# Large expert places in 32-slot products, another order of places, and an fp32 token gather

## The chip, the cores and the metric

The kernel runs on one core of one Trainium2 chip, in one launch. The metric is the time of an execution in device microseconds. Before the change it is 1484.67 us, the median of three runs (1484.15 to 1487.27).

## The reference

A trunk of two layers works on 256 tokens of 1024 features, all in fp32. Layer 0 has attention and a dense SwiGLU. Layer 1 has dilated attention and then the part that matters here, routed experts: each token goes to 2 of 8 experts, and an expert is a SwiGLU with 3584 hidden features. Cut to that part:

```python
logits = jnp.einsum('td,de->te', xt, router)
top_val, top_idx = lax.top_k(logits, TOP_K)          # TOP_K = 2 of 8 experts
gates = jax.nn.softmax(top_val, axis=-1)
...
def one_block(args):
    tok, g, e = args
    xb = xt[tok]
    yb = (jax.nn.silu(xb @ wg[e]) * (xb @ wu[e])) @ wd[e]
    return (yb.astype(jnp.float32) * g[:, None]).astype(h.dtype)
...
y = jnp.zeros_like(xt).at[tok_pad].add(yb.reshape(P, D))
```

An expert has three weight matrices, together 42 MiB in fp32; all eight are read once in each execution, which is 336 loads of 1 MiB.

## The kernel before

**Places.** The experts are worked on one after the other in eight *places*. Place 0 always takes expert 7 (`FIRST`), so that its loads need no routing result; which expert the other places take is decided on the chip by the number of tokens that each expert has. `TWO` lists the small places, which have room for 64 tokens (slots); the other, large ones have 96. `RANK` says which place the expert of each rank gets, so that the three experts with the fewest tokens go to small places. Tokens beyond the room go through `overflow`, which is skipped when there are none.

**A place.** `expert` first makes the hidden features in seven groups of 512: in each, eight steps of 128 input features (`KD`) for gate and up. Then come 28 steps for the output. Each step uses one *granule*, half of a 1 MiB load `w` (128 partitions x 1024 columns); a place has 84 of them, 42 loads. In `products` (L1283 is its matmul) the gathered tokens `xg` are the stationary operand and the weights stream. The slots of a place stand in `parts`: 64 slots as two products side by side in the array, each 64 columns wide, with half of the weight columns (512) each; and in a large place 32 more slots as four products, each 32 wide, with 256 columns each. The 64-slot products write to `psA` (for the output `psD`), the 32-slot ones to `psB`. TensorE executes one fp32 product as two instructions, each with its weight load.

**Around the products.** After a group ScalarE (silu) and VectorE (the product with up) make `hh`, which `turn` transposes on TensorE into `psC` (L1292) and copies to `ht` for the output steps. The call of `turn` in the code stands behind the fourth step of the next group; the order in which instructions stand on an engine is made by a scheduler when the kernel is built. `scatter` scales the result and adds it to the output in DRAM by an indirect DMA on POOL's queue (L1328), one for the 64 slots and in a large place a second one.

**Routing.** Places are gathered in pairs. `route` makes one-hot tiles `oh` (L1242, VectorE) and multiplies the tokens by them (L1251), which puts the tokens of two places into `xg`; smaller products (L1265) give each slot its gate and row. The tokens stand in `htok` twice: rounded to fp32r (L1101), and what the rounding left, also in fp32r (L1152, `htok_lo`); the gather sums the products of both. Route 0 runs ahead of place 0, and the others within the output steps of places 1, 3 and 5.

**Weights.** Loads are issued by SP in the order of use into 16 slots of 1 MiB; a load waits until its slot's last product is done.

Of the kernel before, what the change touches and what calls it, by code (L numbers as in the profile page):

```python
# [10 lines left out]
F32 = mybir.dt.float32  # L11
F32R = mybir.dt.float32r
BF16 = mybir.dt.bfloat16
I32 = mybir.dt.int32
AF = mybir.ActivationFunctionType
ALU = mybir.AluOpType
AX = mybir.AxisListType

P = 128
D = 1024  # L20
# [2 lines left out]
NE = 8  # L23
EPS = 1e-6
BIG = 4096.0
TWO = (1, 3, 5)
FIRST = NE - 1
RANK = (-1, 0, 3, 1, 4, 2, 5, 6)
ROOM = tuple(64 if j in TWO else 96 for j in range(NE))
RING = 8  # L30
NCONV = 3
# [148 lines left out]
def tile_trunk(ctx, tc, xT_d, fm_d, rw_d, ct_d, ada_et, ada_e, win_ab, win_c, uq_d, ukv_d, wout_e,  # L180
# [910 lines left out]
    cms.close()  # L1091
    ring4 = ctx.enter_context(tc.tile_pool(name="ring4", bufs=RING4, side="right"))
    more.append((slot(ring4), RING4))
    htok = keep.tile([P, 2, 2, D], F32R, tag="h", name="htok")
    yt = token_rstd(st, mb)
    lg = mb.tile([P, 2, NE], F32, name="lg")
    for tt in range(2):
        V.scalar_tensor_tensor(lg[:, tt], pl[tt][:, :NE], yt[:, tt:tt + 1], rb, op0=ALU.mult, op1=ALU.add)
    dump("lg", lg)
    for tt in range(2):  # L1100
        S.activation(htok[:, 0, tt], acc[:, tt], AF.Copy, scale=yt[:, tt:tt + 1])  # L1101
    rank = mb.tile([P, 2, NE], F32, name="rank")
    sel = mb.tile([P, 2, NE], F32, name="sel")
    bsh = [P, 2, NE, NE]
# [43 lines left out]
            for j in range(n):  # L1148
                S.copy(t[j * p:(j + 1) * p], g5[j * p:(j + 1) * p, j * w:(j + 1) * w])

    def htok_lo(tt):
        V.scalar_tensor_tensor(htok[:, 1, tt], acc[:, tt], yt[:, tt:tt + 1], htok[:, 0, tt].bitcast(F32),  # L1152
                               op0=ALU.mult, op1=ALU.subtract)

    def tmp3(name):
        return mt.tile([P, 512], F32, tag="xv", name=name, bufs=2)

    iota = C("iota")
    htok_lo(0)
    pos = mb.tile([P, 2, NE], F32, name="pos")  # L1160
    tot = mb.tile([P, 2, NE], F32, name="tot")
    V.tensor_scalar(pos, sel, -4096.0, 4096.0, op0=ALU.mult, op1=ALU.add)
# [34 lines left out]

    def gates():

        htok_lo(1)  # L1200
        V.tensor_reduce(lm, lg, axis=AX.X, op=ALU.max)
        V.tensor_tensor(gate, lg, lm[:, :, None].to_broadcast([P, 2, NE]), op=ALU.subtract)
        S.activation(gate, gate, AF.Exp)
        V.tensor_tensor(gate, gate, sel, op=ALU.mult)
        V.tensor_reduce(gsum, gate, axis=AX.X, op=ALU.add)
        V.reciprocal(gsum, gsum)
        V.tensor_tensor(gate, gate, gsum[:, :, None].to_broadcast([P, 2, NE]), op=ALU.mult)
        placed(gtok[:, :, :, 0], gate, "pg")
        V.tensor_copy(gtok[:, :, :, 1], C("tok")[:, :, None].to_broadcast([P, 2, NE]))
        t = tmp3("pe")[:, :NE * NE].rearrange("p (a b) -> p a b", a=NE)  # L1210
        V.tensor_tensor(t, perm, iota[:, None, :NE].to_broadcast([P, NE, NE]), op=ALU.mult)
        V.tensor_reduce(key, t, axis=AX.X, op=ALU.add)
        V.tensor_copy(eid, key)
        V.tensor_scalar(cap, rk8, float(len(TWO)) - 0.5, -32.0, op0=ALU.is_lt, op1=ALU.mult)
        V.tensor_scalar(cap[:, :NR], cap[:, :NR], 96.0, None, op0=ALU.add)
        V.memset(cap[:, FIRST:FIRST + 1], float(ROOM[0]))
        V.tensor_tensor(ct8, ct8, cap, op=ALU.subtract)
        V.tensor_scalar(ct8, ct8, 0.0, None, op0=ALU.max)
        V.tensor_reduce(cmax, ct8, axis=AX.X, op=ALU.max)
        V.tensor_copy(cnt[:, 0:8], ct8)  # L1220
        V.tensor_copy(cnt[:, 8:9], cmax)

        st_ = C("stri")
        V.tensor_scalar(side[:, 0:1], st_[:, 64:65], -1.0, 2.0 * BIG + 1.0, op0=ALU.mult, op1=ALU.add)
        V.tensor_tensor(side[:, 1:2], st_[:, 32:33], st_[:, 64:65], op=ALU.add)
        V.tensor_tensor(side[:, 1:2], side[:, 1:2], st_[:, 96:97], op=ALU.add)
        V.tensor_scalar(side[:, 1:2], side[:, 1:2], -1.0, 4.0 * BIG + 3.0, op0=ALU.mult, op1=ALU.add)
# [6 lines left out]
    def route(e, hook=lambda: None):  # L1234

        at = (0, ROOM[e])
        n = ROOM[e] + ROOM[e + 1]
        oh = mt.tile([P, 2, 2 * 96], F32R, tag="oh", name="oh")
        xg = xgp.tile([P, KD, 2 * 96], F32, tag="xg", name="xg")
        for tt in range(2):  # L1240
            for i in range(2):
                V.tensor_scalar(oh[:, tt, at[i]:at[i] + ROOM[e + i]], iota[:, :ROOM[e + i]],  # L1242
                                spos[:, tt, e + i:e + i + 1], None, op0=ALU.is_equal)
        hook()
        for a in range(4):
            ps = bank("C").rearrange("p (a b) -> p a b", a=2)
            for b in range(2):
                d = 2 * a + b
                for i in range(2):
                    for tt in range(2):  # L1250
                        TE.matmul(ps[:, b, :n], htok[:, i, tt, d * P:(d + 1) * P], oh[:, tt, :n],  # L1251
                                  start=tt == 0 and i == 0, stop=tt == 1 and i == 1)
            for b in range(2):
                d = 2 * a + b
                S.activation(xg[:, d, :n], ps[:, b, :n], AF.Identity, bias=sh3[:, d:d + 1], scale=gs3[:, d:d + 1])
        back = []
        for i in range(2):
            back.append([])
            for p, (lo, m, q) in enumerate(parts(e + i)):
                gsl = mt.tile([P, 1], F32, tag="gsl", name="gsl", bufs=8)  # L1260
                row = mt.tile([P, 1], I32, tag="row", name="row", bufs=8)
                ps = bank("C")
                for j in range(q):
                    for tt in range(2):
                        TE.matmul(ps[m * j:m * j + m, 0:2], oh[:, tt, at[i] + lo:at[i] + lo + m].bitcast(F32),  # L1265
                                  gtok[:, tt, e + i], start=tt == 0, stop=tt == 1, tile_position=(0, m * j))
                S.copy(gsl, ps[:, 0:1])
                V.scalar_tensor_tensor(row, ps[:, 1:2], float(q), side[:, p:p + 1], op0=ALU.mult, op1=ALU.add)
                back[i].append((gsl, row))
        return xg, at, back  # L1270

    def expert(e, xg, lo, mid, ahead):
# [5 lines left out]
        def products(outs, x, w, m, start, stop):  # L1278
            for ps, (at, n, q) in zip(outs, parts(e)):
                c = 1024 // m // q  # L1280
                wv = w.rearrange("p (m c) -> p m c", m=m)
                for j in range(q):
                    TE.matmul(ps[n * j:n * j + n, :m * c].rearrange("p (m c) -> p m c", m=m), x(at, n),  # L1283
                              wv[:, :, j * c:(j + 1) * c], start=start, stop=stop, tile_position=(0, n * j))

        def turn(g):

# [12 lines left out]
        for g in range(7):  # L1300
            ps = [bank("A"), bank("B")][:len(parts(e))]
            for k in range(KD):
                products(ps, lambda at, n: xg[:, k, lo + at:lo + at + n], next(wg), 2, k == 0, k == KD - 1)
                if g and k == 3:
                    turn(g - 1)
                if g == 0 and k == 3 and mid:
                    mid()
# [51 lines left out]
def overflow(tc, nc, op, e, cap, off, bank, load, ident, htok, gs3, sh3, pos, gate, iota, g5, acc, gu_d, wd_d):  # L1359
# [13 lines left out]
    for a in range(2):  # L1373
        ps = bank("C").rearrange("p (a b) -> p a b", a=4)
        for b in range(4):
            d = 4 * a + b
            for tt in range(2):
                for i in range(2):
                    TE.matmul(ps[:, b], htok[:, i, tt, d * P:(d + 1) * P].bitcast(F32), oh[:, tt],
                              start=tt == 0 and i == 0, stop=tt == 1 and i == 1)  # L1380
        for b in range(4):
            d = 4 * a + b
            V.tensor_scalar(xg[:, d], ps[:, b], gs3[:, d:d + 1], sh3[:, d:d + 1], op0=ALU.mult, op1=ALU.add)
# [59 lines left out]
```

## Time and profile before

| what | value |
|---|---|
| median of three runs | 1484.67 us (1484.15 to 1487.27) |
| profiled execution | 1487.64 us |
| its span (first to last instruction) | 1485.8 us |
| mean granted TensorE clock in it | 0.984 of 2.4 GHz |
| TensorE busy, products | 1418.4 us (95%) |
| VectorE busy | 433.6 us (29%) |
| ScalarE busy | 354.2 us (24%) |
| POOL busy | 51.1 us (3%) |
| read from HBM | 467.34 MB, 317 GB/s over the span |
| first routed products start | 518.3 us into the span |

The profile is of one execution, which took 1.84 us more than its span. Busy time is the sum of instructions, and products overlap, so that 95% does not say that the array is at its peak; which engine holds up the others has to be read stage by stage.

### The profile page before, as it was taken

To read this page: it belongs to the slowest core of one execution; us is meant where nothing else is said; L and a number is where in the kernel's file an instruction comes from. 1 tells how busy PE (TensorE), PEld (TensorE's weight loads), DVE (VectorE), ACT (ScalarE), POOL (GpSimd) and SP (SyncE) were. 2 spreads that over 40 slices of the span, in tenths; PEclk is the share of its full clock that TensorE was granted. 3 is DMA by queue.
4 is the path that set the end of the run, shared out by engine and by line. 5 is a ranking of instruction groups with operands and counts; after the bars stand their busy time and mean duration, and the time that the engine had idled before them with its cause. 6 is when DMAs were issued, how large, how long until landed. Compare 5 with 4: busy or idle time off the path is not lost.

```text
span 1485.8 us, 23384 instructions
## 1 busy us (share of the span) xinstructions
PE 1418.4 (95%) x9779; PEld 647.5 (44%) x9779; DVE 433.6 (29%) x964; ACT 354.2 (24%) x750; POOL 51.1 (3%) x51
## 2 busy tenths in 40 slices
PE   6889999999989899999999998999998999999996
PEld 4646999998766722223322222322222322222221
DVE  5866787786886410000000000000000000000000
ACT  4557644445568310000100001100000100000000
POOL 0320000000020000000000000000000000000000
PEclk9989999999999899999999999999999999999998
DMA  9846678788432788999999999999999999999830
GB/s 393 341 155 251 212 285 299 284 306 308 161 114 91 295 336 321 320 331 415 421 418 420 378 331 419 421 417 421 351 333 410 421 414 421 367 326 335 317 140 11
DMA packets 67363, 472.11 MB, mean 318 GB/s; under 512 B 8145, under 2 KB 8593, under 8 KB 11185
## 3 DMA queue, kind: packets, MB, share of 16 engines
q1 hardware_dynamic: 64944, 467.34, 81.5%
q0 software_dynamic: 1872, 2.10, 0.9%
q8 instruction: 79, 1.29, 0.3%
q10 hardware_dynamic: 432, 1.08, 0.2%
q14 instruction: 36, 0.29, 0.1%
HBM read 467.34 MB, written 3.80 MB: 317 GB/s over the span
## 4 chain that ended last, share of the span: by engine, by line
issue 51%; PE 34%; DMA 7%; DVE 5%; ACT 2%; POOL 0%; POOLq 0%; SPq 0%; ACTq 0%; DVEq 0%
DMA out_dram<-acc,row 7%; PE psA L331 6%; PE psA L332 6%; PE psA L333 6%; PE psA L1283 4%; PE psB L1283 3%; PE psD L1283 2%; DVE wlo L355 1%; PE psD L610 1%; PE psB L315 1%; PE psC L596 1%; PE psB L562 1%; PE psA L562 1%; DMA w<-in_ada_ot_dram 1%; PE psC L1251 0%
## 5 line engine op out<-in xcount | busy, mean ns | idle before, releaser
L1283 PE MATMUL psA<-w,xg 128*64 128x512 f32 x1792 | 453.3, 612 | 0.0
L1283 PE MATMUL psD<-w,ht 128*64 128x512 f32 x896 | 229.3, 611 | 0.0
L1283 PEld LDWEIGHTS psA<-w,xg 128*64 128x64 f32 x1792 | 102.3, 136 | 196.9 <-issue 180.1
L1283 PE MATMUL psB<-w,xg 128*32 128x256 f32 x2240 | 180.8, 393 | 0.0
L1310 ACT ACTIVATE hh<-psA 128x256 f32<-128x256 f32 x56 | 21.5, 384 | 603.3 <-PE psA L1283 603.3
L355 DVE TENSOR_TENSOR wlo<-w,whi 128x1024 fp32r<-128x1024 f32 (+2 forms) x119 | 143.8, 1214 | 44.1 <-ACT whi L353 44.1
L1311 DVE TENSOR_TENSOR hh<-hh,psA 128x256 f32<-128x256 f32 x56 | 23.6, 421 | 452.2 <-ACT hh L1310 452.2
L1283 PEld LDWEIGHTS psB<-w,xg 128*32 128x32 f32 x2240 | 44.4, 108 | 227.7 <-issue 227.7
L353 ACT CAST whi<-w 128x1024 fp32r<-128x1024 f32 (+2 forms) x119 | 122.2, 1038 | 74.1 <-issue 30.0
L331 PE MATMUL psA<-h,whi 128*128 128x256 f32 x352 | 97.1, 277 | 0.2 <-ACT h L455 0.2
L332 PE MATMUL psA<-h,whi 128*128 128x256 f32 x352 | 97.1, 277 | 0.0
L333 PE MATMUL psA<-h,wlo 128*128 128x256 f32 x352 | 96.8, 276 | 0.0
L1283 PE MATMUL psB<-w,ht 128*32 128x256 f32 x1120 | 89.5, 391 | 0.0
L1283 PEld LDWEIGHTS psD<-w,ht 128*64 128x64 f32 x896 | 49.6, 135 | 90.2 <-issue 86.9
L1283 PEld LDWEIGHTS psB<-w,ht 128*32 128x32 f32 x1120 | 22.0, 108 | 113.6 <-issue 109.5
L1327 DVE SCALAR_TENSOR_TENSOR acc<-psD,gsl,g5a 128x512 f32<-128x512 f32 x8 | 6.0, 751 | 224.3 <-PE psD L1283 224.3
L331 PEld LDWEIGHTS psA<-h,whi 128*128 128x128 f32 x352 | 66.0, 188 | 0.6 <-ACT h L455 0.4
L332 PEld LDWEIGHTS psA<-h,whi 128*128 128x128 f32 x352 | 65.9, 188 | 0.3 <-DVE h L456 0.2
L333 PEld LDWEIGHTS psA<-h,wlo 128*128 128x128 f32 x352 | 65.9, 188 | 0.0
L1294 ACT COPY ht<-psC 128x256 f32<-128x256 f32 x56 | 20.9, 372 | 169.7 <-PE psC L1292 169.7
L1328 POOL DMA_INDIRECT out_dram<-acc,row x13 | 20.2, 1557 | 959.0 <-DVE acc L1327 923.4
L1297 DVE COPY ht<-psC 128x128 f32<-128x128 f32 x35 | 10.2, 292 | 141.6 <-ACT ht L1294 141.6
(335 smaller groups left out, 1583.5 us busy)
## 6 DMA issues: line engine op xcount, KB each, us to landing
w<-in_gu_dram SPq DMA_DIRECT2D x224, 1024.0 KB, 10.8
w<-in_wd_dram SPq DMA_DIRECT2D x112, 1024.0 KB, 11.1
w<-in_ada_e_dram SPq DMA_DIRECT2D x22, 1024.0 KB, 8.9
w<-in_ffn_gu_dram SPq DMA_DIRECT2D x22, 1024.0 KB, 5.1
w<-in_ada_ot_dram SPq DMA_DIRECT2D x16, 1024.0 KB, 4.9
w<-in_qkv_dram SPq DMA_DIRECT2D x12, 1024.0 KB, 6.6
w<-in_ffn_d_dram SPq DMA_DIRECT2D x11, 1024.0 KB, 6.6
w<-in_ada_o_dram SPq DMA_DIRECT2D x8, 1024.0 KB, 6.3
```

What stands on the lines that cost most here:

```text
L315: behind(TE.matmul(ps[32 * j:32 * j + 32], sc[:, 4 * i + j], w[:, j], start=i == 0, stop=i == 1, tile_position=(0, 32 * j)), after)
L331: TE.matmul(out_, a[0], b[0], start=start, stop=False)
L332: TE.matmul(out_, a[0], b[1], start=False, stop=False)
L333: TE.matmul(out_, a[1], b[0], start=False, stop=stop)
L353: behind(S.copy(hi[:, :n], w), self.after[0])
L355: self.last = V.tensor_tensor(lw, w, hi[:, :n].bitcast(F32), op=ALU.subtract)
L562: TE.matmul(bk[i][:, tt], q[:, tt * P:(tt + 1) * P], k, start=True, stop=True)
L1283: TE.matmul(ps[n * j:n * j + n, :m * c].rearrange("p (m c) -> p m c", m=m), x(at, n), wv[:, :, j * c:(j + 1) * c], start=start, stop=stop, ...
L1294: S.copy(ht[:, :, 0:64].rearrange("p (j b) t -> p b j t", b=2), pt[:, 0:256].rearrange("p (b j t) -> p b j t", b=2, j=2))
L1310: S.activation(h[:, at:at + w], p[:, 0:w], AF.Silu)
L1311: V.tensor_tensor(h[:, at:at + w], h[:, at:at + w], p[:, w:2 * w], op=ALU.mult)
L1328: G.indirect_dma_start(out=out.rearrange("t (j c) -> (t j) c", j=q), out_offset=bass.IndirectOffsetOnAxis(ap=row[:, 0:1], axis=0), in_=ys, ...
```

## The change

Four things are changed. In `products` the 64 slots of a large place are taken as two times 32, each of the four products with the same 512 weight columns as before; small places keep products that are 64 wide (`b = n if e in TWO else 32`). The small places are 1, 4 and 7 instead of 1, 3 and 5, and `RANK` is rewritten to match. The tokens are kept once, in fp32, so `htok_lo` goes, and the gather multiplies fp32 by fp32, 16 products for a pair of places instead of 32. The call of `turn` stands one step later.

```diff
-TWO = (1, 3, 5)
+TWO = (1, 4, 7)
-RANK = (-1, 0, 3, 1, 4, 2, 5, 6)
+RANK = (-1, 0, 3, 4, 1, 5, 6, 2)
...
-    htok = keep.tile([P, 2, 2, D], F32R, tag="h", name="htok")
+    htok = keep.tile([P, 2, 2, D], F32, tag="h", name="htok")[:, 0]
...
-    def htok_lo(tt):
-        V.scalar_tensor_tensor(htok[:, 1, tt], acc[:, tt], yt[:, tt:tt + 1], htok[:, 0, tt].bitcast(F32),
-                               op0=ALU.mult, op1=ALU.subtract)
...
-        oh = mt.tile([P, 2, 2 * 96], F32R, tag="oh", name="oh")
+        oh = mt.tile([P, 2, 2 * 96], F32, tag="oh", name="oh")
...
-                for i in range(2):
-                    for tt in range(2):
-                        TE.matmul(ps[:, b, :n], htok[:, i, tt, d * P:(d + 1) * P], oh[:, tt, :n],
-                                  start=tt == 0 and i == 0, stop=tt == 1 and i == 1)
+                for tt in range(2):
+                    TE.matmul(ps[:, b, :n], htok[:, tt, d * P:(d + 1) * P], oh[:, tt, :n], start=tt == 0, stop=tt == 1)
...
+                b = n if e in TWO else 32
                 for j in range(q):
-                    TE.matmul(ps[n * j:n * j + n, :m * c].rearrange("p (m c) -> p m c", m=m), x(at, n),
-                              wv[:, :, j * c:(j + 1) * c], start=start, stop=stop, tile_position=(0, n * j))
+                    for i in range(0, n, b):
+                        o = n * j + i
+                        TE.matmul(ps[o:o + b, :m * c].rearrange("p (m c) -> p m c", m=m), x(at + i, b),
+                                  wv[:, :, j * c:(j + 1) * c], start=start, stop=stop, tile_position=(0, o))
...
-                if g and k == 3:
+                if g and k == 4:
                     turn(g - 1)
```

The order of instructions on TensorE in a large place, place 2, around the transposes of a turn, inside a group of gate and up. The numbers behind names tell tiles apart. Before:

```order
L1283 MATMUL psA_7023<-w_7025,xg_6626 64x512 x2
L1283 MATMUL psB_7024<-w_7025,xg_6626 32x256 x4
L1283 MATMUL psA_7023<-w_7025,xg_6626 64x512 x2
L1283 MATMUL psB_7024<-w_7025,xg_6626 32x256 x4
L1292 MATMUL psC_7053<-fm_74,hh_7018 128x128 x3
L1283 MATMUL psA_7023<-w_7039,xg_6626 64x512 x2
L1283 MATMUL psB_7024<-w_7039,xg_6626 32x256 x4
```
and now:

```order
L1278 MATMUL psA_7062<-w_7064,xg_6776 32x512 x4
L1278 MATMUL psB_7063<-w_7064,xg_6776 32x256 x4
L1278 MATMUL psA_7062<-w_7064,xg_6776 32x512 x4
L1278 MATMUL psB_7063<-w_7064,xg_6776 32x256 x4
L1287 MATMUL psC_7110<-fm_74,hh_7057 128x128 x3
L1278 MATMUL psA_7062<-w_7082,xg_6776 32x512 x4
L1278 MATMUL psB_7063<-w_7082,xg_6776 32x256 x4
```
The four instructions 32 wide and 512 columns long have taken the place of two that were 64 wide, and the transposes stand behind two granules of the next group in both.

The second place is the gather on TensorE. Before, it stood within the output steps of a small place; here is its end in the old place 3:

```order
L1251 MATMUL psC_7789<-oh_7750,htok_5398 128x160 x2
L1283 MATMUL psD_7689<-w_7726,ht_7570 64x512 x4
L1251 MATMUL psC_7789<-oh_7750,htok_5398 128x160 x5
L1283 MATMUL psD_7689<-w_7732,ht_7604 64x512 x4
L1251 MATMUL psC_7789<-oh_7750,htok_5398 128x160
L1265 MATMUL psC_7802<-gtok_5503,oh_7750 64x2 x4
L1265 MATMUL psC_7811<-gtok_5503,oh_7750 32x2 x3
```
and now it stands in large places; here is its start in the new place 3:

```order
L1244 MATMUL psC_8543<-oh_8537,htok_5398 128x160
L1278 MATMUL psD_8366<-w_8411,ht_7988 32x512 x4
L1278 MATMUL psB_8367<-w_8411,ht_7988 32x256 x4
L1278 MATMUL psD_8366<-w_8411,ht_7988 32x512 x4
L1278 MATMUL psB_8367<-w_8411,ht_7988 32x256 x4
L1244 MATMUL psC_8543<-oh_8537,htok_5398 128x160 x2
L1278 MATMUL psD_8366<-w_8429,ht_7988 32x512 x4
```
The gather's products now interrupt 32-wide products, one or two at a time at first, and 8 come in a row at the end.

The third place is VectorE's queue ahead of the first route. Before:

```order
L1184 TENSOR_TENSOR pp<-pos,perm 128x128
L1215 TENSOR_SCALAR cap<-cap 128x7
L1216 MEMSET cap 128x1
L1152 SCALAR_TENSOR_TENSOR htok<-acc,ty,htok 128x1024
L1186 TENSOR_REDUCE spos<-pp 128x16
L1152 SCALAR_TENSOR_TENSOR htok<-acc,ty,htok 128x1024
L1242 TENSOR_SCALAR oh<-cl,spos 128x96
L1242 TENSOR_SCALAR oh<-cl,spos 128x64
```
and now:

```order
L1179 TENSOR_TENSOR pp<-pos,perm 128x128
L1209 TENSOR_SCALAR cap<-cap 128x7
L1210 MEMSET cap 128x1
L1181 TENSOR_REDUCE spos<-pp 128x16
L1211 TENSOR_TENSOR ct_5483<-ct_5483,cap 128x8
L1236 TENSOR_SCALAR oh<-cl,spos 128x96
L1236 TENSOR_SCALAR oh<-cl,spos 128x64
L1236 TENSOR_SCALAR oh<-cl,spos 128x96
```
The two operations on `htok` are gone, and one on the counts of tokens (L1211) stands ahead of the first one-hot tile. On SP's queue the loads stand in the same order as before, row by row.

## Rows read from the trace of the kernel before

**Rows 1.** The page: span, and section 1, busy us by engine.
```profile
span 1485.8 us, 23384 instructions
PE 1418.4 (95%) x9779; PEld 647.5 (44%) x9779; DVE 433.6 (29%) x964; ACT 354.2 (24%) x750; POOL 51.1 (3%) x51
```

**Rows 2.** Timeline of POOL: the last place's scatters (start us, us, what).
```profile
1474.09 1.54 POOL L1328 DMA_INDIRECT out_dram<-acc,row  x1 [126.98 <-DVE acc L1327]
1480.69 1.54 POOL L1328 DMA_INDIRECT out_dram<-acc,row  x1 [5.06 <-DMA out_dram<-acc,row]
```

**Rows 3.** Windows cut at the scatters: busy us by engine, clock, DMA share, GB/s.
```profile
662.46:750.22 87.76, 83.38 (x422) 29.34 (x418) 4.75 (x15) 9.11 (x25) 3.27 (x3) 1.00 1.01 410
750.22:885.44 135.22, 135.22 (x1029) 31.93 (x1023) 8.02 (x23) 7.24 (x21) 1.54 (x1) 1.00 0.99 388
885.44:976.55 91.11, 83.90 (x426) 29.54 (x422) 4.92 (x16) 9.10 (x25) 3.09 (x2) 1.00 1.01 413
```

**Rows 4.** Timeline of two large places: four granules, and a turn.
```profile
766.77 1.08 PE L1283 MATMUL psA<-w,xg 128*64 128x512 f32 x4
767.78 0.64 PE L1283 MATMUL psB<-w,xg 128*32 128x256 f32 x8
768.35 1.08 PE L1283 MATMUL psA<-w,xg 128*64 128x512 f32 x4
...
773.08 1.08 PE L1283 MATMUL psA<-w,xg 128*64 128x512 f32 x4
...
991.05 0.55 PE L1292 MATMUL psC<-fm,hh 128*128 128x128 f32 x3
...
991.53 1.08 PE L1283 MATMUL psA<-w,xg 128*64 128x512 f32 x4
```

**Rows 5.** Timeline of a small place: weight loads of two rounds, then a turn's.
```profile
697.75 0.14 PEld L1283 LDWEIGHTS psA<-w,xg 128*64 128x64 f32 x2 [0.29 <-issue]
698.18 0.14 PEld L1283 LDWEIGHTS psA<-w,xg 128*64 128x64 f32 x2 [0.29 <-issue]
...
700.15 0.20 PEld L1292 LDWEIGHTS psC<-fm,hh 128*128 128x128 f32 x2 [1.82 <-DVE hh L1311]
```

**Rows 6.** Timeline: weight loads of 32-wide quads, first and last of four.
```profile
502.39 0.13 PEld L315 LDWEIGHTS psA<-w,sc 128*32 128x32 f32 x4 [0.30 <-issue]
...
503.68 0.13 PEld L315 LDWEIGHTS psA<-w,sc 128*32 128x32 f32 x4 [0.30 <-issue]
```

**Rows 7.** Gather in a small place: timeline, then the group of psC (durations min/median/max).
```profile
950.76 0.63 PEld L1251 LDWEIGHTS psC<-oh,htok 128*128 128x128 f32 x5 [0.81 <-issue]
...
L1251 PEld LDWEIGHTS psC<-oh,htok x32: 186/192/192, 943.4 to 961.1; 128*128 128x128 f32 x32
```

**Rows 8.** Start of the first route: timeline, then windows as in rows 3.
```profile
507.66 1.28 DVE L1152 SCALAR_TENSOR_TENSOR htok<-acc,ty,htok 128x1024 fp32r<-128x1024 f32 x1
...
510.24 0.77 DVE L1242 TENSOR_SCALAR oh<-cl,spos 128x96 fp32r<-128x96 f32 x4
510.81 7.22 PE L1251 MATMUL psC<-oh,htok 128*128 128x160 f32 x32 [4.01 <-DVE oh L1242]
...
500.00:510.00 10.00, 6.29 (x50) 2.89 (x48) 6.56 (x31) 3.73 (x6) 0.70 (x1) 1.00 0.96 367
510.00:520.00 10.00, 9.19 (x44) 7.70 (x44) 2.84 (x20) 3.50 (x9) 0.00 (x0) 0.51 1.01 426
```

**Rows 9.** DMA issues from 530 us (count, KB, us to landing); packets from 700 to 830.
```profile
w<-in_gu_dram SPq DMA_DIRECT2D x207, 1024.0 KB, 11.6
w<-in_wd_dram SPq DMA_DIRECT2D x112, 1024.0 KB, 11.1
...
DMA packets 7612, 54.60 MB, mean 420 GB/s; under 512 B 900, under 2 KB 900, under 8 KB 972
...
w<-in_gu_dram SPq DMA_DIRECT2D x28, 1024.0 KB, 19.9
```

**Rows 10.** Window of the dense feed-forward, columns as in rows 3.
```profile
200.00:300.00 100.00, 100.00 (x880) 100.00 (x880) 79.00 (x128) 49.72 (x73) 0.00 (x0) 1.00 0.79 289
```

More of the change, by code (lines that the diff above doesn't have):

```diff
@@ L1100, in tile_trunk @@
     for tt in range(2):
-        S.activation(htok[:, 0, tt], acc[:, tt], AF.Copy, scale=yt[:, tt:tt + 1])
+        S.activation(htok[:, tt], acc[:, tt], AF.Copy, scale=yt[:, tt:tt + 1])
     rank = mb.tile([P, 2, NE], F32, name="rank")
@@ L1158, in tile_trunk @@
     iota = C("iota")
-    htok_lo(0)
     pos = mb.tile([P, 2, NE], F32, name="pos")
@@ L1198, in gates @@
     def gates():
-        htok_lo(1)
         V.tensor_reduce(lm, lg, axis=AX.X, op=ALU.max)
@@ L1264, in route @@
                     for tt in range(2):
-                        TE.matmul(ps[m * j:m * j + m, 0:2], oh[:, tt, at[i] + lo:at[i] + lo + m].bitcast(F32),
+                        TE.matmul(ps[m * j:m * j + m, 0:2], oh[:, tt, at[i] + lo:at[i] + lo + m],
                                   gtok[:, tt, e + i], start=tt == 0, stop=tt == 1, tile_position=(0, m * j))
@@ L1377, in overflow @@
             for tt in range(2):
-                for i in range(2):
-                    TE.matmul(ps[:, b], htok[:, i, tt, d * P:(d + 1) * P].bitcast(F32), oh[:, tt],
-                              start=tt == 0 and i == 0, stop=tt == 1 and i == 1)
+                TE.matmul(ps[:, b], htok[:, tt, d * P:(d + 1) * P], oh[:, tt], start=tt == 0, stop=tt == 1)
         for b in range(4):
```

## The prediction

> **What bounds the kernel now.** I read the page's totals first: TensorE is busy 95% of a 1485.8 us span, VectorE and ScalarE under 30% [rows 1]. Since that is an average over stages of different limits, I then cut the span at the scatters that end the expert places, from 662.46 to 1474.09 us [rows 2, 3]. Three of the rows stand there; all seven give 87.8, 91.1 and 91.2 us for the small places and 135.2 (three times) and 135.9 for the large ones. That is 812 us, over half of the kernel, and nearly everything the diff touches is in it and in the first place before it.
>
> What ends last in a place? In a large place TensorE never pauses (135.22 busy of 135.22) while 388 GB/s arrive; in a small place it is 410 to 413, the DMA engines are full, and TensorE is still busy 84 of 91 us [rows 3]. So TensorE sets the pace of a large place. In a small one slots come free faster than they fill, and still what TensorE waits for there is not weights: the row of a transpose names DVE's hh [rows 5].
>
> The timeline of a large place shows what a granule (half of a 1 MiB load) costs: the two 64-slot products start 1.01 us before the four 32-slot ones, and those 0.57 us before the next granule; four granules take 6.31 us, 1.577 each [rows 4]. The instruction counts are double because one fp32 product is two instructions. 84 x 1.577 = 132.5 us; with seven groups of transposes that is the place. Yet the same pair of 64-slot products in a small place, where nothing 32 wide stands between, starts a new round every 0.43 us, 0.86 us for its two rounds [rows 5]. So of the 1.01 us, 0.15 us is not streaming but the change of tile width; the 0.57 us of the 32-slot part should hold a like amount, since half as many columns in two rounds ask 0.43.
>
> **The change part by part.** *Two times 32 in large places.* Every product of a large place becomes 32 wide, so the width no longer changes within or between granules. Is a quad of 32-wide, 512-column products as fast as a pair of 64-wide ones? The trace has that shape: the conditioning products of L315, of which four quads load their weights from 502.39 to 503.68, 0.43 us apart [rows 6]. So the 64-slot part costs 2 x 0.43 = 0.86 us. The 32-slot part isn't shown without a width change; its bounds are 0.43 (half of the 512-column quads' 0.86) and today's 0.57. I take 0.43, as the quads of L315 stream at exactly the pace of the pairs. The granule is then 1.29 us instead of 1.577, and 5 places x 84 x 0.288 = **-121 us**. The other bound of the 64-slot part too is today's (1.01), which gives no gain.
>
> The Trainium skill has a rule against this, in "TensorE: Matmul & The Clock Gate", What overlaps and what doesn't: weight loads overlap running products only when the row group differs, and tiles side by side in columns share it. By it each of four rounds would pay its 0.13 us load, the granule would be 1.81 us and the kernel some 98 us slower. The trace disagrees: rounds follow at 0.43 us with a load in each, 0.13 to 0.14 us long [rows 5, 6].
>
> *Transposes.* Three per turn take 0.48 us from the first to the next product [rows 4]. That includes a width change which the 32-to-64 step had to pay anyway; now both of its changes are its own. I add 0.14 us (0.57 - 0.43) x 7 x 5 = **+4.9 us**. In the new order a turn stands two granules behind its group as before (five in place 0), and 2 x 1.29 us of products cover the way over ACT and DVE to hh. Without cover that way shows in a small place: the load at 698.18 serves the round at 698.61, the next is due at 699.04, and the transposes come at 700.15, 1.1 us late [rows 5]. So it has 1.5 us to spare. Small places keep that wait, in three places before and after: 0.
>
> *Gather.* Hi and lo in fp32r were 32 products of 0.11 us (five loads take 0.63 us, the last of them 0.19) [rows 7], 3.5 us per pair of places. Now there are 16 fp32 products of two instructions each. 160 columns at 0.43 per 512 are 0.134 us each, 192 are 0.161: 4.3 or 5.2 us. Three routes, one of them with 192: **+3.2 us**. Below, 0.11 would be the bound (0); above, a doubling (+10). Routing for places 4 and 6 moves from small into large places, where it isn't free, but it wasn't free before: 91.1 us less 82 (72 of products, 10 of turns) leaves about 9 us in a small place. The gather interrupts the products as often as before, 8 times; 0, within 3 us either way.
>
> *Start.* Two DVE operations of 1.28 us go from ahead of the one-hot tiles, whose first then comes about 2.2 us sooner; TensorE waits for just that (4.01 us) [rows 8]. The first gather runs at the low clock: granted 0.51 in 510 to 520 us [rows 8], that is 1.2 GHz, after a stretch in which TensorE was 63% busy. There its 32 products take 7.22 us; twice 0.134 x 32 is 8.6, +1.4. Net **-1 us** (0 to -4, if the clock rises sooner).
>
> *Order of places, tail.* The counts of both kinds stay 5 and 3, so the sum of TensorE work doesn't change by order. But the last place is small and ends in one scatter. Now the second waits for the first's landing: issue at 1474.09, again at 1480.69, end 1485.8 [rows 1, 2]. One scatter goes: **-5.1 us** (to -6.6, by the first one's time).
>
> SP's queue keeps its rows and order, slots their number. What is late next is DMA, so I check it. After 530 us 319 loads are still issued [rows 9]. At 420 GB/s one (1.049 MB) takes 2.497 us: 796 us, ending at 1327, plus about 10 for the last granules and scatter: 1337. The new sum is 1367 us in span, so 30 us remain. A large place of 135.2 - 24.2 + 1.0 = 112 us would ask a load per 2.67 us, slower than DMA gives. A small one takes 82 us where DMA needs 105; the 23 us must be in the ring, which holds 16 loads (40 us), some 8 of them in flight when it is short (19.9 us to landing) [rows 9]. That cover is thin, but full after a large place. Were it gone, each small place would cost up to 23 us.
>
> The sum: -121 + 4.9 + 3.2 - 1 - 5.1 = -119.0. The profiled execution took 1487.64 us, 1.84 beyond its span and 2.97 above the median of the runs. It would become 1368.6, and the median 1484.67 - 119 = 1365.7: **1366 us**.
>
> **The rivals.**
> - *DMA becomes the bound.* If four streams at once slow the writes, or the ring is short in small places. At 2.63 us a load (5% more) the 319 end at 1369, the span at 1379: 1378 on the median's scale; local starvation of 5 to 10 us per small place gives 1375 to 1395. For it: a small place now runs DMA at its ceiling for 90 us on end and 30 us is the whole slack. Against it: 420 GB/s held from 700 to 830 us, over half of that under a large place's products [rows 9]. Its time: 1383.
> - *Half the gain.* The step from 512- to 256-column quads costs what the width change cost at one of its two edges, 0.14 us per granule. 420 x 0.14 = 59: 1425 us. For it: no row shows this alternation without a width change. Against it: quads follow each other freely at L315, and nothing there hints at a price for their length.
> - *Slower: TensorE's instruction supply.* A large granule goes from 24 instructions (weight loads and products) to 32. If the supply has a pace over 49 ns, 32 of them last longer than 1.577 us, and from there on the change loses. The densest long stretch, 200 to 300 us, has 1760 in 100 us, 57 ns each [rows 10]: at that pace a granule is 1.82 us, +0.24 x 420 = +101, and +2 for the rest: 1588 us. Against it: there each product streams 256 columns, which explains the pace without any limit; and 32-slot parts already start 16 instructions in 0.57 us, 35 ns each, if only in bursts. The Trainium skill, "TensorEngine Tiling (Array Packing)", Instruction Overhead, gives about 60 cycles per matmul; added to each of 16 without overlap, that is an estimated 0.4 us a granule and 1534 us. By that rule quads would come at a slower pace than pairs; the trace shows 0.43 us for both and does not agree [rows 5, 6].
> - *Weight loads in the open.* Each of a granule's four rounds pays its load, 0.13 us [rows 6]: 1.81 us, +98 for the granules in place of -121, 1585 us. Against it is every round of a small place [rows 5].
> - *It doesn't do what it says.* Rounds of quads within a place don't shorten at all, the 1.01 and 0.57 stay: +3.2 for the gather, -6.1 for start and tail: 1482.
>
> **How the numbers follow.** My forecast 0.68, with a range of its own of 1354 to 1380 (the gather's, the start's and the tail's bounds, and the routing's 3 us); DMA 0.13; half the gain 0.10; instruction supply 0.06; weight loads 0.01; no effect 0.02. The time is that of the first, 1366. A range that leaves no more than 2 in 10 out takes the forecast's and the DMA cases: 1352 to 1400. A measurement of this kernel tells 0.2%, 3 us, from no change: faster 0.92 (the first three, and half of the last), same 0.01, slower 0.07.
>
> **What would show it.** Right: scatters 111 to 113 us apart after places 2 and 6, 120 to 122 where routing has moved (3 and 5), about 82 in places 4 and 7; a large granule of 1.29 us; DMA at 390 GB/s or more in large places; transposes of large places without a wait. Wrong: a granule of 1.43 (half the gain) or over 1.58 (supply); TensorE's idle time put down to DMA of w in small places (starvation); the end more than 7 us behind the last scatter's issue. The step that I trust least is the 0.43 us of the 256-column quads.

## The result, and the profile after

The changed kernel takes 1362.20 us (median of four runs, 1360.05 to 1365.29), the kernel before, run beside it, 1485.93 (1484.15 to 1487.27). The ratio is 0.917, 95% interval 0.9144 to 0.9195: 8.3% faster. 1366 was forecast, 1352 to 1400 the range. The profiled execution is the longest of the four, 1365.29 us with a span of 1363.4.

The page after, its totals and the DMA lines of the slices, answers to [rows 1]:

```profile
span 1363.4 us, 26743 instructions
PE 1303.9 (96%) x11459; PEld 721.5 (53%) x11459; DVE 428.8 (31%) x962; ACT 354.0 (26%) x750; POOL 51.1 (4%) x51
...
GB/s 391 369 150 204 291 223 279 280 302 305 311 160 123 33 263 423 420 381 410 421 421 417 420 420 411 421 420 390 403 420 417 421 420 420 412 420 419 408 422 219
```

TensorE still looks like the only bound, with 114.5 us less work. But from the sixteenth slice to the last but one the DMA engines now bring 381 to 423 GB/s. Windows cut at the scatters of the places, as in [rows 3] (places 1 to 7, counted from 0 here and below; us, busy of PE, PEld, DVE, ACT, POOL, clock, DMA share, GB/s):

```profile
634.51:722.31 87.80, 83.87 (x442) 30.44 (x442) 5.04 (x16) 9.46 (x26) 3.27 (x3) 1.00 1.02 417
722.31:834.72 112.41, 112.41 (x1365) 44.96 (x1361) 7.40 (x23) 7.22 (x21) 1.53 (x1) 1.00 1.01 419
834.72:956.19 121.47, 121.47 (x1429) 54.01 (x1423) 8.69 (x31) 11.04 (x32) 3.09 (x3) 1.00 1.00 409
956.19:1039.58 83.39, 76.80 (x364) 24.95 (x364) 3.81 (x9) 5.29 (x14) 3.08 (x2) 1.00 1.02 414
1039.58:1160.84 121.26, 121.26 (x1431) 50.60 (x1427) 7.87 (x26) 11.03 (x32) 1.55 (x2) 1.00 1.01 419
1160.84:1273.52 112.68, 112.68 (x1363) 45.86 (x1357) 7.51 (x24) 7.23 (x21) 3.08 (x2) 1.00 1.02 417
1273.52:1356.89 83.37, 75.71 (x348) 24.48 (x344) 3.82 (x9) 5.29 (x14) 3.09 (x2) 1.00 0.89 364
```

Large places take 112.4 and 112.7 us, those with the routing 121.5 and 121.3; TensorE does not pause in them. In the small places 4 and 7 it is busy 76 to 77 of 83.4 us. What fills the difference is in the waits (us in total, times, longest):

```profile
PEld psC L1287 <- DVE hh L1306: 33.6, 19, 1.8
PE psC L1287 <- DVE hh L1306: 16.0, 17, 0.9
...
PEld psA L1278 <- DMA w<-in_gu_dram: 3.1, 12, 0.3
```

A turn's first weight load waits up to 1.8 us for `hh`, and TensorE itself is idle for 0.9 of that. In the windows of places 4 and 7 each of the 14 turns has such a gap; in place 1 four of the seven have it, and the other three stand later in the next group and wait for nothing. Weights are waited for in trifles only. The granules of a large place, in the timeline of PE, answer to [rows 4]:

```profile
736.00 1.04 PE L1278 MATMUL psA<-w,xg 128*32 128x512 f32 x8
736.85 0.61 PE L1278 MATMUL psB<-w,xg 128*32 128x256 f32 x8
737.28 1.04 PE L1278 MATMUL psA<-w,xg 128*32 128x512 f32 x8
738.14 0.61 PE L1278 MATMUL psB<-w,xg 128*32 128x256 f32 x8
```

The 512-column quads start 0.85 us before the 256-column ones, and those 0.43 before the next granule: 1.28 to 1.29 us, with twice the instructions of [rows 4] in the 64-slot part. The end, in POOL's timeline: one scatter, issued at 1356.89, 6.5 us ahead of the span's end; before, the first of two was issued 11.7 us ahead of it [rows 1, 2].

```profile
1356.89 1.54 POOL L1323 DMA_INDIRECT out_dram<-acc,row  x1 [72.08 <-DVE acc L1322]
```

So the span's 122.4 us came from three stretches: 27.9 (27.95) from what lies ahead of the first scatter (662.46 before, 634.51 after), 89.2 from there to the last place's (811.6, 722.4), 5.2 from the end.

### The profile page after: what moved, and what is told of

Same layout as the page of the kernel before. It is cut to its first block, busy times and chain, and to the rows that moved or that the text cites. A ratio compares the mean times of both kernels' runs of the same rounds, so it can differ in the third digit from the quotient of the medians.

```text
span 1363.4 us, 26743 instructions
## 1 busy us (share of the span) xinstructions
PE 1303.9 (96%) x11459; PEld 721.5 (53%) x11459; DVE 428.8 (31%) x962; ACT 354.0 (26%) x750; POOL 51.1 (4%) x51
## 4 chain that ended last, share of the span: by engine, by line
PE 87%; DVE 6%; issue 3%; ACT 2%; DMA 1%; POOL 0%; POOLq 0%; SPq 0%; ACTq 0%; DVEq 0%
PE psA L1278 28%; PE psD L1278 15%; PE psB L1278 13%; PE psA L331 7%; PE psA L332 6%; PE psA L333 6%; PE psC L1287 2%; PE psC L1244 2%; DVE wlo L355 1%; PE psD L610 1%; PE psB L315 1%; DMA w<-in_wd_dram 1%; PE psC L596 1%; PE psB L562 1%; PE psA L562 1%
## 5 line engine op out<-in xcount | busy, mean ns | idle before, releaser
L1278 PE MATMUL psA<-w,xg 128*32 128x512 f32 (+1 forms) x2912 | 445.8, 594 | 0.0
L1278 PE MATMUL psD<-w,ht 128*32 128x512 f32 (+1 forms) x1456 | 227.0, 594 | 0.0
L1278 PEld LDWEIGHTS psA<-w,xg 128*32 128x32 f32 (+1 forms) x2912 | 118.4, 116 | 139.4 <-issue 89.9
L1278 PEld LDWEIGHTS psB<-w,xg 128*32 128x32 f32 x2240 | 74.3, 110 | 165.0 <-issue 163.4
L1278 PEld LDWEIGHTS psD<-w,ht 128*32 128x32 f32 (+1 forms) x1456 | 63.3, 116 | 68.2 <-issue 46.9
L331 PE MATMUL psA<-h,whi 128*128 128x256 f32 x352 | 98.6, 281 | 0.2 <-ACT h L455 0.2
L332 PE MATMUL psA<-h,whi 128*128 128x256 f32 x352 | 98.6, 282 | 0.0
L1278 PE MATMUL psB<-w,ht 128*32 128x256 f32 x1120 | 95.1, 379 | 0.0
L1278 PEld LDWEIGHTS psB<-w,ht 128*32 128x32 f32 x1120 | 40.1, 110 | 77.7 <-issue 75.1
```

The costliest lines, as they stand in the source:

```text
L331: TE.matmul(out_, a[0], b[0], start=start, stop=False)
L332: TE.matmul(out_, a[0], b[1], start=False, stop=False)
L1278: TE.matmul(ps[o:o + b, :m * c].rearrange("p (m c) -> p m c", m=m), x(at + i, b), wv[:, :, j * c:(j + 1) * c], start=start, stop=stop, til ...
```

## The experiments

The theory at first: the width change, 0.14 us at each edge, was all that large places lost; the rest of the change is worth a few us; transfers have room. The rivals: 32-wide tiles are faster in themselves, or gather and order of places carry much of the gain. There are twelve runs; each result is the median, the ratio to the kernel before that was run beside it, and the ratio's 95% interval.

**The split alone**, in the kernel before: its gather, its order of places.

```
+                b = n if e in TWO else 32
...
+                    for i in range(0, n, b):
+                        o = n * j + i
```

> The kernel before with one edit, the 64 slots of large places as two times 32; places, gather and call of the turn as before. Theory (the gain is the changes of tile width that go): -121 us for granules and +4.9 for turns, 1370 us within 5; large places 112 us apart, small ones 88 to 91 as before. Rival (the order of places, with its effect on the weight loads, and the gather bring most of it): within 30 us of before, above 1455.

1377.82 us, ratio 0.9284 (0.9263 to 0.9305): the split carries 108 of the 124 us. It missed the expectation by some 8 us, more than the 5 allowed. Place 5, small in the old order, shows why. Its window, and the weight loads in it (timeline of PEld):

```profile
1037.84:1138.28 100.44, 87.66 (x436) 28.51 (x436) 4.45 (x13) 9.46 (x26) 3.09 (x3) 0.98 1.02 419
```

```profile
1086.49 0.20 PEld L1286 LDWEIGHTS psA<-w,xg 128*64 128x64 f32 x4 [1.43 <-DMA w<-in_gu_dram]
1088.98 0.20 PEld L1286 LDWEIGHTS psA<-w,xg 128*64 128x64 f32 x4 [1.43 <-DMA w<-in_gu_dram]
```

It takes 100.4 us, where place 3, small too, takes 90.9. In most of the stretch from 1057 to 1100 us and again from 1130 us to its end, loads are waited for, and the products that wait follow each other 2.49 us apart. In the old order, with small places 1, 3 and 5, one large place stands between two small ones, which would be too little to refill the slots: a theory for the run with the old order below. The prediction had priced the order at 0.

**Everything but the split** (`b = n` in the changed kernel).

> The changed kernel with the 64 slots of large places in one product again; places, gather and call of the turn as changed. Theory: the change's time plus 116, 1478 us within 5, with 1.58 us per large granule. Rival (order and gather bring most of it): under 1400 us.

1473.56 us, 0.9921 (0.9905 to 0.9938): 12.5 us less than the kernel before, as expected, and 9.6 more than the prediction's terms for it (+3.2 - 1 - 5.1). Most of that lies at the start: from POOL's last work on `ty` ahead of the routing to the first scatter it takes 152.8 us (500.10 to 652.93), the kernel before 160.2 (502.28 to 662.46). Its trace has no low clock at the first gather; more on that under the old gather.

**Half of the width changes**, in the kernel before: 64-slot and 32-slot products swap their order in each granule, so that equal widths meet.

```
+            turned[0] ^= 1
-            for ps, (at, n, q) in zip(outs, parts(e)):
+            for ps, (at, n, q) in list(zip(outs, parts(e)))[::1 if turned[0] else -1]:
```

> The kernel before, with products as wide as before, but every second granule takes its 32-slot products first, so that the width changes twice per two granules and not four times. Theory (a pair of width changes costs 0.288 us): 210 pairs fewer, -60 us, 1425 us within 8. Rival (32-wide products are faster in themselves, the width change is free): no difference, 1486 us.

1433.01 us, 0.9641 (0.9621 to 0.9661): 53 us from half of the changes (60 were expected), no product narrower. Timeline of PE:

```profile
759.69 1.03 PE L1286 MATMUL psA<-w,xg 128*64 128x512 f32 x4
760.65 1.07 PE L1286 MATMUL psB<-w,xg 128*32 128x256 f32 x16
761.65 1.94 PE L1286 MATMUL psA<-w,xg 128*64 128x512 f32 x8
763.52 0.85 PE L1286 MATMUL psB<-w,xg 128*32 128x256 f32 x12
```

Two granules' 32-slot parts take 1.00 us from start to start, four rounds of 0.215 and one change of 0.14; two 64-slot parts 1.87, four rounds of 0.43 and 0.15. The granule is 1.435, halfway between 1.577 and 1.29.

**32 wide everywhere**, small places too (`b = 32`).

> The changed kernel with small places 32 wide as well. Theory: there a pair and a quad both take 0.43 us a round and no width change goes within a small place, so no difference beyond 3 us from the change, 1362 us. Rival (32-wide products are faster in themselves): three small places get shorter, by 5 us or more each, 1347 us or less. Rival (instruction supply is near its limit): small places get longer.

1362.33 us, 0.9167 (0.915 to 0.9185): no difference. The time alone would not settle it, since a small place also waits for `hh` and for loads. The pace of its products does. A group's eight granules between two turns of place 4, in the timeline of PE, first in the changed kernel and then in this run:

```profile
972.27 7.09 PE L1278 MATMUL psA<-w,xg 128*64 128x512 f32 x32
...
972.71 7.07 PE L1278 MATMUL psA<-w,xg 128*32 128x512 f32 x64
```

Narrow tiles aren't faster; not changing is.

**More instructions**: in large places each 512-column quad is issued as two of 256, but for the first and last step of a sum.

```
+                if n == 64 and b == 32 and not (start or stop):
+                    for z in range(2):
...
+                            TE.matmul(ps[o:o + 32, z * 256:z * 256 + 256], ...,
```

> The changed kernel, in which each 512-column product of 64 slots in a large place is given as two of 256 columns, but for the first and last step of each sum: 48 products a granule in place of 32 in 340 of the 420 large granules, the same columns. If the width of columns sets the pace (0.43 us for a round of four of 512, 0.215 us for a round of four of 256, and both rows stand in the trace): 1362 us, plus or minus 4, granule 1.29 us. Rival, a pace set by the number of instructions, at the 40 ns each that 32 in 1.29 us make: granule 1.94 us, and 1362 + 340 x 0.65 = 1580 us. In between, a limit of 30 ns each would give 1.44 us and 1413 us.

1365.57 us, 0.9203 (0.9173 to 0.9233): as expected. The expectation's 48 and 32 "products" are instructions, products and their weight loads together. Timeline of PE:

```profile
759.74 1.04 PE L1286 MATMUL psA<-w,xg 128*32 128x512 f32 x8
760.60 0.61 PE L1286 MATMUL psB<-w,xg 128*32 128x256 f32 x8
761.03 1.05 PE L1279 MATMUL psA<-w,xg 128*32 128x256 f32 x16
761.90 0.61 PE L1286 MATMUL psB<-w,xg 128*32 128x256 f32 x8
```

16 product instructions of 256 columns take 0.87 us from start to start, 8 of 512 take 0.86. The windows give 114.75 us for the large place that took 112.41: 68 such granules, 34 ns each for 8 more products and 8 more loads. The rival of an instruction pace is out: 48 instructions, products and loads together, go by in 1.3 us, 27 ns each. The Trainium skill, "TensorEngine Tiling (Array Packing)", Instruction Overhead, gives about 60 cycles per matmul. Read as a time added to each, as in the prediction, 8 more would be an estimated 0.2 us a granule; the trace, at 0.03 us, does not agree with that reading. The page's own example, a product of one column that takes as long as one of 60, can also be read as a shortest time, which the granules' products of 256 and 512 columns do not test.

**The old order of places** in the changed kernel, formed as a theory after the first run: the order is worth the tail's 5 us and the starvation's 10.

```
-TWO = (1, 4, 7)
+TWO = (1, 3, 5)
-RANK = (-1, 0, 3, 4, 1, 5, 6, 2)
+RANK = (-1, 0, 3, 1, 4, 2, 5, 6)
```

> The changed kernel with small places 1, 3 and 5 as before. Theory as revised after the first four runs (in that order the slots run empty in place 5, TensorE waits for weights there by some 10 us, and a second scatter ends the kernel, 5 us): 1377 us within 4. Rival, the prediction's term (the order moves the tail alone): 1367 us.

1376.17 us, 0.9249 (0.9221 to 0.9278): as expected, 14.0 us slower than the new order. Place 5 again takes 100.4 us (1037.78 to 1138.20).

**Half the bytes.** Loads bring half of their columns and both granules of a load use that half, so half of the weights are left out. First with the old places, then with the new.

```
-            return lambda: load(wd_d[FIRST, pc].rearrange("p a b -> p (a b)"), (2048,))
+            return lambda: load(wd_d[FIRST, pc].rearrange("p a b -> p (a b)")[:, :1024], (1024,))
...
-            for lo in (0, 1024):
+            for lo in (0, 0):
```

> As the run before, but each weight load brings only the first half of its columns, and both granules use that half, so that the DMA has half the bytes and TensorE the same products (part of the computation is left out). Theory: the 10 us of place 5 go, 1367 us within 4, small place 5 about as long as place 3. Rival (place 5 is long for another reason): no change against the run before.

> The changed kernel with half the bytes in each weight load, both granules using that half (part of the computation is left out). Theory (TensorE bounds the changed kernel in every place, the DMA is nowhere waited for): 1362 us within 3. Rival (the DMA bounds part of it): 1355 us or less.

1346.07 us, 0.9059 (0.9032 to 0.9086), and 1341.00 us, 0.9022 (0.8998 to 0.9047). Both missed by 21 us. Their difference is 5.1 us, the tail's price: with half the bytes the other 9 of the 14.0 us between the two orders are gone, so they were waits for loads. The second run seemed to say that transfers cost the changed kernel 21 us, though hardly a wait of it names them. The instruction order showed another way: with shorter loads a small place's transposes had come to stand behind the fifth granule of the next group, no longer directly behind their own (in place 4 the first one starts 4.2 us after ScalarE's work on its group does, in the changed kernel 0.9), and the waits for `hh` were gone from the list of both. Each of the two runs had changed two things. The next three runs take them apart.

**The later turn alone**, with all bytes: in small places the transposes are held behind the granule at which `turn` is called.

```
-                TE.transpose(pt[:, b * P:(b + 1) * P], h[:, b * P:(b + 1) * P], ident)
+                behind(TE.transpose(pt[:, b * P:(b + 1) * P], h[:, b * P:(b + 1) * P], ident),
+                       done[0] if e in TWO else None)
```

> The changed kernel with the transposes of small places held behind the granule after which the code calls them, so that they don't wait for hh. TensorE saves 1.1 us in each of 19 turns, 21 us. Theory (the DMA is what comes next: the last load lands 5 us before its use): part of it, 1345 to 1357 us, with TensorE waiting for w in small places. Rival (the slots cover it): 1341 us.

1358.66 us, 0.914 (0.9112 to 0.9167): 3.5 us faster than the changed kernel, with intervals that overlap, and 1.7 outside the expected range. The waits for `hh` are gone and others stand in their place:

```profile
PEld psD L1280 <- DMA w<-in_wd_dram: 13.8, 12, 1.5
PE psD L1280 <- DMA w<-in_wd_dram: 5.2, 10, 0.7
```

Windows of its small places 4 and 7, and two weight loads in place 7 (timeline of PEld):

```profile
950.94:1029.49 78.55, 76.36 (x353) 24.45 (x353) 3.82 (x9) 5.29 (x14) 3.09 (x2) 1.00 1.02 416
...
1264.90:1351.11 86.21, 78.31 (x348) 23.40 (x344) 3.82 (x9) 5.30 (x14) 3.09 (x2) 1.00 0.92 376
```

```profile
1325.83 0.20 PEld L1280 LDWEIGHTS psD<-w,ht 128*64 128x64 f32 x4 [1.41 <-DMA w<-in_wd_dram]
1328.31 0.20 PEld L1280 LDWEIGHTS psD<-w,ht 128*64 128x64 f32 x4 [1.43 <-DMA w<-in_wd_dram]
```

Place 4 gains 4.8 us of its 83.4 and place 7 loses 2.8: there, for a stretch, the products come at the pace of the loads, 2.48 us apart.

**The early turn held, half the bytes**: each small place's transposes stand directly behind their group.

```
+            if g and e in TWO:
+                turn(g - 1)
```

> The changed kernel with loads of half the columns (both granules of a load use the same half, so half the weights are left out), and in the three small places the transposes of a group held directly behind the group, where the changed kernel has them; in the earlier run with half the bytes they had moved behind five granules of the next group and the wait of 1.8 us for hh was gone. If that shift alone made the earlier run 21 us faster and the transfers are hidden in the changed kernel: 1362 us, plus or minus 4, with 21 waits of 1.1 to 1.8 us for hh. Rival: the transfers cost the changed kernel those 21 us in a way that its waits do not show: 1341 us, plus or minus 4, with the waits for hh in the trace all the same.

1359.92 us, 0.916 (0.9138 to 0.9182): as expected. The waits for `hh` are there, and in all 21 turns, three more than leave TensorE idle in the changed kernel (place 1):

```profile
PE psC L1290 <- DVE hh L1313: 19.7, 21, 0.9
```

**The later turn, half the bytes.**

> The run with the later turn of the small places (1358.66 us), with loads of half the columns (half the weights are left out), so that its places of transposes are the ones written down by hand and the transfers can't be late. If its gain of only 3.5 us is because the transfers then become the bound: 1341 us, plus or minus 4 (the waits of TensorE for w, 13.8 + 5.2 + 5.3 + 1.0 us by its list of waits, gone, and the small places fifth and eighth at 76 us). Rival, the later turn itself is worth only those 3.5 us and the other 18 of the first run with half the bytes came from its other shifts of instructions: 1358 us, plus or minus 4.

1339.65 us, 0.9019 (0.8999 to 0.9039): as expected. From the first scatter on the list of waits names no transpose that waits for `hh` and no weights; windows of places 4 and 7:

```profile
944.62:1020.95 76.33, 76.33 (x364) 24.95 (x364) 3.81 (x9) 5.29 (x14) 3.08 (x3) 1.00 0.86 287
1252.68:1328.98 76.30, 75.22 (x348) 24.48 (x344) 3.82 (x9) 5.29 (x14) 3.09 (x2) 1.00 0.58 192
```

The four together (us, medians):

| | all bytes | half the bytes | what transfers cost |
|---|---|---|---|
| turn directly behind its group | 1362.20 | 1359.92 | 2.3 |
| turn behind five granules | 1358.66 | 1339.65 | 19.0 |
| what the wait for `hh` costs | 3.5 | 20.3 | |

Neither cost can be read from one row or column alone: the wait for `hh` hides most of the transfers' shortage, and with it gone the shortage appears. The small numbers, 2.3 and 3.5, come from runs whose intervals overlap, and the three more waits of the run with the early turn held (0.9 us each) would make the 2.3 about 5. With the turn behind five granules as tried here, the changed kernel has some 3.5 us to gain until its loads hold it up; another order of places wasn't tried with it.

**The old gather** in the changed kernel: hi and lo in fp32r again.

```
-    htok = keep.tile([P, 2, 2, D], F32, tag="h", name="htok")[:, 0]
+    htok = keep.tile([P, 2, 2, D], F32R, tag="h", name="htok")
...
+    htok_lo(0)
```

> The changed kernel with the gather of before put back: tokens kept as a rounded part and a rest, four fp32r products for each piece of the gather in place of two fp32 ones. The prediction priced the new gather at +3.2 us and the shorter start at -1 us (0 to -4). By the trace after, where TensorE fell to the low clock for only 3.4 us at the first gather, and before, where it did for 17 us, the start was worth some 4 us more. If the start is what counts: 1366 us, plus or minus 3 (1366 = 1362.2 + 4 + 3.2 - 3.2), with the long stretch of low clock back. Rival, by the prediction's own two terms: 1360 us (1362.2 + 1 - 3.2), with no long stretch of low clock.

1363.65 us, 0.9187 (0.916 to 0.9214), 1.4 more than the changed kernel with intervals that overlap: the time decides for neither. (The theory's own terms, 1362.2 + 1 + 4 - 3.2, give 1364 and not the 1366 that was written.) The traces do. From POOL's last work on `ty` to the first scatter, first this run and then the changed kernel, in windows; and place 3, large with routing, in this run, where the changed kernel takes 121.47:

```profile
500.15:636.51 136.36, 131.84 (x1475) 56.10 (x1469) 19.17 (x80) 18.34 (x44) 0.70 (x1) 0.95 1.00 391
503.64:634.51 130.87, 128.56 (x1475) 54.51 (x1469) 17.13 (x78) 18.32 (x44) 0.70 (x1) 0.99 1.01 408
...
835.26:955.95 120.69, 120.63 (x1429) 53.71 (x1423) 8.68 (x31) 11.05 (x32) 3.09 (x3) 1.00 1.01 412
```

So the new start is worth 5.5 us, and the new gather costs 0.8 in each of the large places 3 and 5 (0.78 and 0.80). Here too the instruction order moved: one turn each in places 1 and 4 stands later than in the changed kernel and saves its wait of 0.9 us. These two waits and the gather bring the 5.5 us down to about the 1.4 that the medians show.

The clock goes with the start. The timeline of PE gives the first gather, here and then in the changed kernel, and the windows of this run the clock around it:

```profile
508.69 7.21 PE L1251 MATMUL psC<-oh,htok 128*128 128x160 f32 x32 [4.01 <-DVE oh L1242]
...
509.97 4.09 PE L1244 MATMUL psC<-oh,htok 128*128 128x160 f32 x16 [1.79 <-DVE oh L1236]
```

```profile
505.00:510.00 5.00, 1.31 (x6) 1.29 (x6) 5.00 (x24) 0.44 (x2) 0.00 (x0) 0.80 1.01 423
510.00:515.00 5.00, 5.00 (x25) 5.00 (x25) 0.55 (x4) 2.49 (x6) 0.00 (x0) 0.50 1.03 433
515.00:520.00 5.00, 5.00 (x39) 1.99 (x38) 0.32 (x2) 1.17 (x5) 0.00 (x0) 0.50 1.00 419
520.00:525.00 5.00, 5.00 (x58) 2.38 (x59) 0.88 (x5) 0.16 (x1) 0.00 (x0) 0.83 1.02 421
```

In the changed kernel's windows the low clock, 0.5 or 1.2 GHz, is over within the second of these rows:

```profile
505.00:510.00 5.00, 2.69 (x23) 0.87 (x15) 4.45 (x31) 2.73 (x5) 0.00 (x0) 1.00 0.98 375
510.00:515.00 5.00, 5.00 (x19) 3.91 (x19) 2.10 (x14) 1.72 (x4) 0.00 (x0) 0.66 1.03 433
515.00:520.00 5.00, 5.00 (x70) 3.83 (x73) 0.44 (x4) 2.08 (x7) 0.00 (x0) 1.00 1.00 423
```

Ahead of the gather TensorE stood idle for 4.01 us in the one and for 1.79 in the other. It holds beyond this pair: in the four profiled kernels with the old gather (before among them) the idle time is 4.01 us and the mean clock from 500 to 535 us is 0.76 to 0.80; in the ten with the new gather it is 1.78 or 1.79 us, and the mean clock is 0.95 in three and 1.00 in seven.

## Why the prediction was right, step by step

- **Granules.** 1.577 to 1.29 us, the forecast's number, the 0.43 us of the 256-column quads (least trusted) included. Large places without routing came out at 112.4 to 112.7 against 112.0. That the gain is the width change itself, and lies in its edges, is shown by half of the changes giving half of it, and by narrow tiles giving nothing in small places. Why an edge costs 0.14 us no run shows; that the products go to `psA` and `psB` in turn is not it, since they still do. "Half the gain" and the "instruction supply" are out by the timelines, "weight loads in the open" by the same 0.43 us steps.
- **Transposes.** The forecast added 0.14 us a turn, since a change to the transposes' width and back is now all their own. Most of it is there: 0.55 us pass from the start of the last 32-slot products to that of the transposes, 0.12 more than pass to the next granule where no turn stands between (0.43), and the 0.48 behind them are as before (timeline of PE, place 2):

```profile
755.53 0.61 PE L1278 MATMUL psB<-w,xg 128*32 128x256 f32 x8
756.08 0.55 PE L1287 MATMUL psC<-fm,hh 128*128 128x128 f32 x3
756.56 1.06 PE L1278 MATMUL psA<-w,xg 128*32 128x512 f32 x8
```

- **Routing, gather.** Two small places lost the routing and 7.7 us each (91.1 to 83.4; 9 was the estimate), two large ones gained it and 8.8 (121.4 against 112.5). Of the difference, 1.1 us, 0.8 is the new gather's price by the run with the old one, as the forecast had it for a pair of 160 slots; the 0.3 left is the move itself. For the pair of 192, forecast at 1.7, place 1 shows less: 1.5 us between the two runs, of which 0.9 is a wait for `hh`. The small places' waits for `hh` stay, as said.
- **Start.** This term is mis-sized: -1 us (0 to -4) was forecast, and -5.3 was measured. From POOL's last work on `ty` to the first scatter it was 160.2 us before and is now 130.9. The split alone brings it to 136.1 (499.61 to 635.73 in that run), and the last 5.3 come with the new gather; putting the old one back costs 5.5. The one-hot tiles did come 2.2 us sooner, as forecast (TensorE idle for 1.79 us, not 4.01). What failed is the +1.4: the gather was priced at the low clock throughout, 8.6 us, and its two halves take 4.09 and 2.44, since the clock rose within the first. The products behind it run at the full clock too.
- **Tail.** 11.7 to 6.5 us: -5.2, forecast -5.1.
- **Sum.** -119 was forecast, -122.4 the two spans give, -123.7 the medians. The start, 4.3 us more than its term, more than covers the distance; against it a large place without routing got 22.8 us shorter (135.2 to 112.4), not 23.2.
- **Order of places.** The step that failed, without harm to the number. It was put at 0, since "the sum of TensorE work doesn't change by order". The sum does not, but when slots run empty does: the new order avoids a starvation of some 9 us (14.0 measured, less 5.1 for the tail) that the split alone runs into. The prediction looked for it only in the order that the change has. That its 0 did no harm to the number is luck: in the old order the same reasoning would have been 9 us out.
- **Transfers.** "30 us remain" was wrong: by the runs of the table the later turn gains 3.5 us, not 20, and the rest turns into waits for weights. The forecast let the last load land at 1327; windows of the changed kernel show transfers until about 1349:

```profile
600.00:1340.00 740.00, 722.90 (x7057) 283.97 (x7051) 44.82 (x136) 56.93 (x161) 18.69 (x12) 1.00 1.01 415
1340.00:1349.00 9.00, 9.00 (x44) 3.02 (x42) 0.00 (x0) 0.00 (x0) 0.00 (x0) 1.00 0.72 298
1349.00:1356.00 7.00, 6.82 (x32) 2.01 (x28) 0.14 (x1) 0.00 (x0) 0.00 (x0) 1.00 0.01 2
```

The 319 loads counted by issue left out those in flight at 530 us and the 2 MB of the scatters (10 us together, by 420 GB/s), and the mean is 415 and less at the end, not 420. The rival "DMA becomes the bound" was much nearer than 0.13 let a reader think; saving a few us more of TensorE time in the small places met it (the later turn alone).

## What to carry to other kernels

Where products of two tile widths alternate, time the step between starts within one width and across the change; here an edge costs 0.14 us. Giving the wide product as two narrow ones removes it, and the narrow ones run at the same pace. When an engine is sped up, compare the time at which its last transfer would land with the time at which the engine would then be done, with every byte counted, and ask in which order stages draw on the slots: an order that was free before can starve. And when a suspected cost is taken away and the time moves by another amount than expected, look whether the instruction order moved too before believing either number; two waits that hide each other need the table with both. To say what an engine did ahead of an event, read the timeline up to the event: a window that reaches over it counts the event's own work.

## What the runs showed of the hardware

- A change between 64-wide and 32-wide column tiles costs 0.14 to 0.15 us each way; within one width rounds follow every 0.43 us at 512 columns and every 0.215 at 256, each with its weight loads.
- Halving the columns and doubling the products leaves the time nearly as it is (34 ns a granule for 8 more products and their loads).
- Where TensorE waits for each 1 MiB load, the products that wait follow each other 2.48 to 2.49 us apart (place 5 of the split alone, with 419 GB/s over the place, and place 7 of the run with the later turn).
- The first gather's low clock (1.2 GHz) went with how long TensorE stood idle ahead of it: after 4.01 us it lasted some 14 us in the run with the old gather, after 1.79 us 3.4 in the changed kernel, and in seven other profiles none is seen. That the one causes the other wasn't tried by itself.
